# Four blocks of 256 channels for the modulation's shift and scale, with the first two products run beside them

## The chip, the cores and the metric

The kernel runs on one core of a Trainium2 chip. The metric is the device time of one launch in microseconds (us). The kernel before took 747.63 us in the median of 3 runs (746.4 to 748.59). The profile shown here is one further execution, of 750.78 us.

## The reference

One layer of a hybrid transformer over 256 latent tokens and 256 context tokens of 1024 channels. What matters here is its beginning; all else (two attentions, a Fourier mix, a convolution, a merge, a mixture of 16 experts) stays as it is.

```
m  = silu(c) @ w_mod + b_mod              # 6 x 1024 columns: sh1, sc1, g1, sh2, sc2, g2
mc = silu(c_ctx) @ w_mod + b_mod          # the same for the context tokens
h  = rms_norm(x,   norm1_g) * (1 + sc1)  + sh1
hc = rms_norm(ctx, norm1_g) * (1 + csc1) + csh1
gq, gk, gv, nq, nk, nv, fu, cu, gl = split(h @ w_in)      # w_in: 1024 x 7936, products of 256 columns each
```

So the shift `sh1` and the scale `sc1` need the first 2048 columns of `w_mod`, over all 1024 rows (8 MB in 32 bits). The two products `gq` (512 columns of `w_in`, two pieces of 256) are the first that read `h`.

## The kernel before

All of `h` lies transposed: 8 channel tiles k of 128 channels, each with 256 tokens. Every product of the first part runs in three passes with high and low parts: `h` is split by ScalarE (cast, `hhi`) and VectorE (difference, `hlo`), and a weight tile of 1 MB (8 channel tiles by 256 columns) likewise, in two halves of four channel tiles (`stream`, lines 266 to 278; lines 275 and 276 are the cast and the difference). A product of 256 columns is 48 matmuls of 256 columns: 2 halves of the tokens, 8 channel tiles, 3 passes.

The weights come on SyncE's DMA queue (SP), one issue of 1 MB at a time, into a pool `wp` of 4 buffers. An issue waits until its buffer is free, and whatever stands behind it on SP waits too. The constants (`pk`) and `x` (`xs`) come on ScalarE's DMA queue at the same time. A scheduler puts each engine's instructions into a fixed order before the run; an engine waits at the head of its order.

The beginning: `mod_set(0)` (lines 157 to 176) loads the 2048 columns in 8 tiles of 128 rows with 2048 columns (line 162), and adds for each tile 4 matmuls of 512 columns that sit side by side in the four column groups of TensorE (line 164). Only after the eighth tile is the sum complete. Then it is copied out (line 169), turned by 4 transposes (line 172), the bias is added (line 174), and `sh1` and `a1` (which is norm1_g times one plus the scale) come out for all 8 channel tiles at once (lines 248 and 249). `turned_norm` has by then normalized `x` (line 216) and transposed it (line 221). `modulated` (lines 228 to 241) makes `h` channel tile by channel tile: VectorE for the even tiles (line 235), ScalarE for the odd ones (line 237), the cast (line 238), the difference (line 239). The weights of the first `gq` product are loaded behind the 8 tiles; GpSimd makes their low parts. The two `gq` products (line 388) follow, then the context tokens are loaded, normalized, turned and modulated (line 391), then the product `gkv` of both kinds of tokens, and `cb`, `ca`, `nk` and so on.

`side_work` runs one step of `rest_of_mod` after each product from the second on: each step loads another 1 MB of `w_mod` (`wv`, line 184), and VectorE adds it up (lines 190 and 192).

Of the kernel before, what the change touches and what calls it, by code (L numbers as in the profile page):

```python
# [9 lines left out]
F32 = mybir.dt.float32  # L10
F32R = mybir.dt.float32r
# [3 lines left out]
ALU = mybir.AluOpType  # L15
# [37 lines left out]
def mixer_moe(ctx: ExitStack, tc: tile.TileContext, A, out, dbg=None):  # L53
    nc = tc.nc
    V, SC, G, PE = nc.vector, nc.scalar, nc.gpsimd, nc.tensor

    def dump(name, ap):
        if dbg is not None and name in dbg:
            nc.gpsimd.dma_start(dbg[name], ap)
# [12 lines left out]
    def pt(tag, name):  # L72
        return banks["pool"].tile([P, 512], F32, tag=tag, bufs=banks["n"][tag], name=name)
# [7 lines left out]
    def tr_t(name):  # L81
        return pt("tr", name)
# [46 lines left out]
    def big(name, dt=F32):  # L129
        return hp.tile([P, 2048], dt, tag="h", name=name)  # L130
# [21 lines left out]
    V.scalar_tensor_tensor(cth, cth, 1.0, cc, op0=ALU.add, op1=ALU.mult)  # L152
    V.tensor_scalar_mul(csil[:, :, 0:2], cth, 0.5)

    bm = pks("bm").rearrange("p (s j b) -> p s j b", s=3, j=4)

    def mod_set(s, out):

        acc = pt("md", f"mod{s}")
        for k in range(NK):  # L160
            wm = wp.tile([P, 2048], F32, tag="w", name=f"wm{s}_{k}")
            nc.sync.dma_start(wm, A["w_mod"][k * P : (k + 1) * P, 2048 * s : 2048 * (s + 1)])
            for j in range(4):
                PE.matmul(acc[32 * j : 32 * j + 32, :], csil[:, k, :], wm[:, 512 * j : 512 * (j + 1)],
                          start=(k == 0), stop=(k == NK - 1))
            yield
        m = t2(f"m{s}")
        for h in range(2):
            (V.tensor_copy if h else SC.copy)(m[:, 256 * h : 256 * h + 256], acc[:, 256 * h : 256 * h + 256])
        t = tr_t(f"mt_{s}")  # L170
        for b in range(4):
            PE.transpose(t[:, 128 * b : 128 * (b + 1)], m[:, 128 * b : 128 * (b + 1)], ident)
        mt = small.tile([P, 4, 4, 2], F32, name=f"mc_{s}", tag="mc", bufs=2)
        V.tensor_tensor(mt.rearrange("p j b r -> p b j r"), t.rearrange("p (b j r) -> p b j r", b=4, j=4)[:, :, :, 0:2],
                        bm[:, s].rearrange("p j b -> p b j").unsqueeze(3).to_broadcast([P, 4, 4, 2]), op=ALU.add)
        out.append(mt)

    def mod_sums(i, res):

# [48 lines left out]
    def modulated(xT, r, name):

        hi = big(f"hhi{name}", F32R).rearrange("p (k t) -> p k t", k=NK)  # L230
        lo = big(f"hlo{name}", F32R).rearrange("p (k t) -> p k t", k=NK)
        for k in range(NK):
            f = xT[:, k, :]
            if k % 2 == 0:
                V.tensor_scalar(f, f, a1[:, k, r : r + 1], sh1[:, k, r : r + 1], op0=ALU.mult, op1=ALU.add)
            else:
                SC.activation(f, f, AF.Identity, scale=a1[:, k, r : r + 1], bias=sh1[:, k, r : r + 1])
            SC.copy(hi[:, k, :], f)
            V.tensor_sub(lo[:, k, :], f, hi[:, k, :].bitcast(F32))
        dump(f"h{name}", hi.bitcast(F32))  # L240
        H.append((hi, lo))

    xlT = turned_norm(xs, big("xn").rearrange("p (t d) -> p t d", t=NT), big("xTl"), "l")
    mc = []
    for _ in mod_set(0, mc):
        pass
    mc0 = mc.pop()
    V.tensor_copy(sh1, mc0[:, 0:2].rearrange("p j b r -> p (j b) r"))
    V.scalar_tensor_tensor(a1, mc0[:, 2:4].rearrange("p j b r -> p (j b) r"), 1.0,
                           pks("n1g").unsqueeze(2).to_broadcast([P, NK, 2]), op0=ALU.add, op1=ALU.mult)  # L250


    aside = []
# [40 lines left out]
    def tok_major(X, t):  # L294
        return lambda k, w, xi: (X[xi][:, k, 128 * t : 128 * (t + 1)], w)
# [1004 lines left out]
```

## Time and profile before

| what | before |
|---|---|
| median of 3 runs | 747.63 us (746.4 to 748.59) |
| profiled execution, its span | 750.78 us, 749.0 us |
| TensorE matmul busy | 643.1 us (86%) |
| VectorE busy | 414.1 us (55%) |
| ScalarE busy | 265.8 us (35%) |
| GpSimd busy | 71.0 us (9%) |
| moved by DMA | 180.06 MB, mean 240 GB/s |
| granted TensorE clock, mean | 0.942 |

How to read it: a row of a timeline has the start in us from the span's start, the duration in us, the engine, the line of the kernel, the operation, what it writes and reads, the count, and in brackets the engine's idle time before it with what ended it. Neighbouring instructions of one kind are merged into a row. PE is TensorE, PEld its weight loads, DVE VectorE, ACT ScalarE, POOL GpSimd, SP SyncE; a q behind a name is its queue. A granted clock of 1.00 is 2.4 GHz, 0.50 is 1.2 GHz. Buffer numbers are left out of names, so `gq` stands for both products and `wm` for all tiles of `w_mod`.

### The profile page before, as it was taken

Reading aid. Unit: us, or ns where it says so; the run is one execution under the profiler, and the core shown is the slowest. Engines: PE = TensorE matmul, PEld = TensorE weight load, DVE = VectorE, ACT = ScalarE, POOL = GpSimd, SP = SyncE. Lnnn points to the kernel's source line nnn. Section 1 sums busy time; section 2 is a strip of 40 time slices with the busy share of each in tenths; the row PEclk is TensorE's granted clock in tenths of the full one; section 3 lists DMA queues with packets and bytes.
Section 4 is the critical chain, followed back from the end, with each engine's and each line's share of the span. In section 5 each row is a group of like instructions: output and inputs, shape, how many; then the busy total and the mean of one; then the engine's idle time right before and its main releaser. Section 6 shows DMA issues by size and latency. Waiting matters only on the chain. (4 is left out here: it accounts for less than half of the span.)

```text
span 749.0 us, 12068 instructions
## 1 busy us (share of the span) xinstructions
PE 643.1 (86%) x4725; PEld 444.3 (59%) x4725; DVE 414.1 (55%) x806; ACT 265.8 (35%) x486; POOL 71.0 (9%) x112
## 2 busy tenths in 40 slices
PE   3689899999999999999999686879789778797882
PEld 0278899978887999898999522423224224232221
DVE  0279799988988766775666523431324324304233
ACT  1157845367556343434545311220102112201011
POOL 1134200022111002112120100000000000000000
PEclk9979999999999999999999878989899999999995
DMA  9895653542624878577984608999658999966002
GB/s 365 295 330 158 194 171 113 180 158 71 205 85 163 295 254 265 198 249 258 320 296 171 225 1 322 408 407 408 257 226 359 406 408 408 381 246 267 1 2 87
DMA packets 75119, 180.06 MB, mean 240 GB/s; under 512 B 3104, under 2 KB 39072, under 8 KB 74016
## 3 DMA queue, kind: packets, MB, share of 16 engines
q1 hardware_dynamic: 73088, 172.90, 63.3%
q0 software_dynamic: 1104, 3.15, 1.3%
q10 hardware_dynamic: 848, 2.94, 1.0%
q8 instruction: 52, 0.85, 0.5%
q14 instruction: 27, 0.22, 0.1%
HBM read 177.92 MB, written 1.05 MB: 239 GB/s over the span
## 5 line engine op out<-in xcount | busy, mean ns | idle before, releaser
L810 PE MATMUL gu<-we,hg 128*32 128x512 f32 x832 | 111.0, 655 | 3.2 <-PEq L1125 3.2
L288 PE MATMUL gl<-hhil,wl_gl 128*128 128x256 f32 x256 | 72.8, 286 | 1.5 <-DVE wl_gl L276 1.4
L810 PEld LDWEIGHTS gu<-we,hg 128*32 128x32 f32 x832 | 29.6, 117 | 74.2 <-issue 71.4
L288 PE MATMUL gl<-hhil,wh_gl 128*128 128x256 f32 x256 | 73.4, 287 | 0.0
L288 PE MATMUL gl<-hlol,wh_gl 128*128 128x256 f32 x256 | 72.4, 283 | 0.0
L456 DVE SCALAR_TENSOR_TENSOR cv<-zp,pk,cv 128x256 f32<-128x256 f32 x120 | 51.2, 477 | 0.2
L275 ACT CAST wh_gl<-w_gl 128x1024 fp32r<-128x1024 f32 x32 | 33.1, 1048 | 50.0 <-PE gl L288 25.2
L810 PE MATMUL y<-we,hT 128*32 128x512 f32 x416 | 49.6, 607 | 0.9 <-PEq L1176 0.8
L288 PEld LDWEIGHTS gl<-hhil,wl_gl 128*128 128x128 f32 x256 | 48.1, 189 | 3.7 <-DVE wl_gl L276 3.1
L288 PEld LDWEIGHTS gl<-hhil,wh_gl 128*128 128x128 f32 x256 | 48.1, 188 | 1.6 <-issue 1.6
L288 PEld LDWEIGHTS gl<-hlol,wh_gl 128*128 128x128 f32 x256 | 48.2, 188 | 0.5 <-issue 0.5
L288 PE MATMUL z<-y,wh_br 128*128 128x256 f32 x256 | 47.6, 283 | 0.0
L276 DVE TENSOR_TENSOR wl_gl<-w_gl,wh_gl 128x1024 fp32r<-128x1024 f32 x32 | 41.0, 1294 | 9.8 <-ACT wh_gl L275 9.6
L192 DVE SCALAR_TENSOR_TENSOR acc<-wv,csil,acc 128x512 f32<-128x512 f32 x56 | 41.1, 762 | 6.5 <-DMA wv<-in_w_mod_dram 6.4
L288 PEld LDWEIGHTS z<-y,wh_br 128*128 128x128 f32 x256 | 39.6, 188 | 0.9 <-issue 0.7
L874 DVE TENSOR_TENSOR si<-si,gu 128x256 f32<-128x256 f32 x16 | 6.6, 418 | 59.4 <-ACT si L873 59.3
L288 PE MATMUL z<-y,wl_br 128*128 128x256 f32 x128 | 36.8, 289 | 1.8 <-DVE wl_br L276 1.7
L372 ACT CAST yh<-ys 64x512 fp32r<-64x512 f32 x32 | 19.7, 616 | 46.3 <-DVE ys L892 45.7
L873 ACT ACTIVATE si<-gu 128x256 f32<-128x256 f32 x16 | 6.0, 383 | 84.1 <-PE gu L810 65.7
L810 PEld LDWEIGHTS y<-we,hT 128*32 128x32 f32 x416 | 14.2, 111 | 31.3 <-issue 29.5
L892 DVE SCALAR_TENSOR_TENSOR ys<-y,gsl,G 128x512 f32<-128x512 f32 x16 | 12.0, 751 | 34.6 <-PE y L810 31.2
L672 POOL TENSOR_TENSOR merged<-merged,gt 128x512 f32<-128x512 f32 x12 | 19.3, 1610 | 117.6 <-DVE gt L671 117.6
(411 smaller groups left out, 1525.5 us busy)
## 6 DMA issues: line engine op xcount, KB each, us to landing
we<-in_w_gu_dram SPq DMA_DIRECT2D x64, 1024.0 KB, 9.7
we<-in_w_down_dram SPq DMA_DIRECT2D x32, 1024.0 KB, 15.8
wv<-in_w_mod_dram SPq DMA_DIRECT2D x16, 1024.0 KB, 5.5
w_gl<-in_w_in_dram SPq DMA_DIRECT2D x16, 1024.0 KB, 5.6
wm<-in_w_mod_dram SPq DMA_DIRECT2D x8, 1024.0 KB, 9.4
w_br<-in_w_branch_dram SPq DMA_DIRECT2D x8, 1024.0 KB, 5.2
w_out<-in_w_out_dram SPq DMA_DIRECT2D x4, 1024.0 KB, 5.4
w_gq<-in_w_in_dram SPq DMA_DIRECT2D x2, 1024.0 KB, 8.3
```

What stands on the lines that cost most here:

```text
L192: V.scalar_tensor_tensor(acc[:, s], wm[:, k % 2, s], csil[:, k, 0:1], acc[:, s], op0=ALU.mult, op1=ALU.add)
L275: SC.copy(w[0], raw[:, s])
L276: sub(w[1], raw[:, s], w[0].bitcast(F32), op=ALU.subtract)
L288: PE.matmul(dst, a, b, start=(k == 0 and wi + xi == 0), stop=(k == kt - 1 and wi == 1))
L372: SC.copy(hi, src)
L456: V.scalar_tensor_tensor(cv[:, ct, :], zp[:, ct, j : j + S], convw[:, ct, j : j + 1], cv[:, ct, :], op0=ALU.mult, op1=ALU.add)
L672: G.tensor_tensor(mt, mt, gts[c], op=ALU.add)
L810: tc.keep_in_program_order(PE.matmul(*a, **k))
L873: SC.activation(si, acc[:, :n], AF.Silu)
L874: V.tensor_tensor(si, si, acc[:, n:], op=ALU.mult)
L892: V.scalar_tensor_tensor(ys, y, gsl, G2[flip], op0=ALU.mult, op1=ALU.mult)
```

## The change

The shift and the scale are made in four blocks of 256 channels (two channel tiles). A block b loads two tiles: the 256 shift columns and the 256 scale columns, over all 1024 rows (`mod_load`, the same 1 MB each, now in pieces of 1 KB per row instead of 8 KB). `mod_product` runs 32 matmuls of 128 columns into the four column groups where 4 per tile of 512 columns ran before (128 matmuls in all where there were 32, for the same columns), and VectorE copies 128 columns out. `mod_turn` transposes once and writes two channel tiles of `sh1` and `a1` with three small VectorE operations. `modulated` is called for these two channel tiles. The two `gq` products are cut up by channel tiles: `first_products(c, ks)` adds the channel tiles ks of product c, for tiles of `h` that were made one block earlier, and the last two channel tiles come at the end. Each of the four accumulators (2 pieces of columns, 2 halves of tokens) now has a bank of its own, three of the pool `mm`, one of `sc`. The second product's weights lie in two buffers of the pool `h` (`wide`). The loads of the two `gq` weight tiles stand behind block 0 and block 1. The counter that starts `side_work` is set to 2 by hand, so that the first step of `rest_of_mod` comes after `gkv`.

```diff
+    def mod_load(b):
+        ws = []
+        for i in range(2):
+            wm = wp.tile([P, 2048], F32, tag="w", name=f"wm{b}_{i}").rearrange("p (k n) -> p k n", k=NK)
+            c = D * i + 2 * P * b
+            nc.sync.dma_start(wm, A["w_mod"][:, c : c + 2 * P].rearrange("(k p) n -> p k n", p=P))
+            ws.append(wm)
+        return ws
+
+    def mod_product(b, ws):
+        acc = pt("md", f"mod{b}")
         for k in range(NK):
-            wm = wp.tile([P, 2048], F32, tag="w", name=f"wm{s}_{k}")
-            nc.sync.dma_start(wm, A["w_mod"][k * P : (k + 1) * P, 2048 * s : 2048 * (s + 1)])
-            for j in range(4):
-                PE.matmul(acc[32 * j : 32 * j + 32, :], csil[:, k, :], wm[:, 512 * j : 512 * (j + 1)],
+            for g in range(4):
+                PE.matmul(acc[32 * g : 32 * g + 32, :P], csil[:, k, :], ws[g // 2][:, k, P * (g % 2) : P * (g % 2) + P],
                           start=(k == 0), stop=(k == NK - 1))
+        m = t2(f"m{b}")
+        V.tensor_copy(m[:, :P], acc[:, :P])
+        return m
+
+    def mod_turn(b, m):
+        t = tr_t(f"mt_{b}")
+        PE.transpose(t[:, :P], m[:, :P], ident)
...
+        V.tensor_tensor(sh1[:, k, :], t[:, 0], bias[:, 0, k].unsqueeze(2).to_broadcast([P, 2, 2]), op=ALU.add)
+        V.tensor_tensor(mt, t[:, 1], bias[:, 1, k].unsqueeze(2).to_broadcast([P, 2, 2]), op=ALU.add)
+        V.scalar_tensor_tensor(a1[:, k, :], mt, 1.0, pks("n1g")[:, k].unsqueeze(2).to_broadcast([P, 2, 2]),
+                               op0=ALU.add, op1=ALU.mult)
...
-    ws0 = stream(A["w_in"][:, :256], NK, "gq0", G.tensor_tensor)
-    modulated(xlT, 0, "l")
+    new_h("l")
+    gq = [[(sc_t if 2 * c + t == 3 else mm_t)(f"gq{c}{t}")[:, :256] for t in range(NT)] for c in range(2)]
+    gws = []
+
+    def first_products(c, ks):
+        for t in range(NT):
+            for k in ks:
+                w = gws[c][2 * k // NK]
+                for wi, xi in ((0, 0), (0, 1), (1, 0)):
+                    a, b = tok_major(H[0], t)(k, w[wi][:, k % 4, :], xi)
+                    PE.matmul(gq[c][t], a, b, start=(k == 0 and wi + xi == 0), stop=(k == NK - 1 and wi == 1))
+
+    for b in range(4):
+        m = mod_product(b, mod_load(b))
+        if b:
+            first_products(0, range(2 * b - 2, 2 * b))
+        mod_turn(b, m)
+        if b < 2:
+            gws.append(stream(A["w_in"][:, 256 * b : 256 * b + 256], NK, f"gq{b}", V.tensor_tensor if b else G.tensor_tensor, b == 1))
+        modulated(xlT, 0, range(2 * b, 2 * b + 2))
+        if b:
+            first_products(1, range(2 * b - 2, 2 * b))
+    for c in range(2):
+        first_products(c, range(6, NK))
+    n_prod[0] = 2
...
-    gq = [in_cols(256 * c, f"gq{c}", tok_major, ws=None if c else ws0)[0] for c in range(2)]
...
-    modulated(turned_norm(ctxs, ctxs, big("xTc"), "c"), 1, "c")
+    new_h("c")
+    modulated(turned_norm(ctxs, ctxs, big("xTc"), "c"), 1, range(NK))
```

What the change moves on the engines is shown at three places. First SyncE's queue from its start. Before, the eight tiles of `w_mod` go ahead of both `gq` weight tiles, one tile of `wv` and the context tokens (`wm0_3` is the fourth tile):

```order
L162 DMA wm0_0_141<-in_w_mod_dram 128x2048
L162 DMA wm0_1_147<-in_w_mod_dram 128x2048
...
L162 DMA wm0_7_183<-in_w_mod_dram 128x2048
L270 DMA w_gq0_201<-in_w_in_dram 128x8x256
L270 DMA w_gq1_297<-in_w_in_dram 128x8x256
L184 DMA wv4_0_356<-in_w_mod_dram 128x2x1024
L390 DMA ctxs_360<-in_ctx_dram 128x2x1024
L270 DMA w_gkv_491<-in_w_in_dram 128x8x256
```

Now (`wm3_1` is the scale tile of block 3):

```order
L161 DMA wm0_0_146<-in_w_mod_dram 128x8x256
L161 DMA wm0_1_148<-in_w_mod_dram 128x8x256
L273 DMA w_gq0_191<-in_w_in_dram 128x8x256
L161 DMA wm1_0_207<-in_w_mod_dram 128x8x256
L161 DMA wm1_1_209<-in_w_mod_dram 128x8x256
L273 DMA w_gq1_264<-in_w_in_dram 128x8x256
L161 DMA wm2_0_290<-in_w_mod_dram 128x8x256
L161 DMA wm2_1_292<-in_w_mod_dram 128x8x256
L161 DMA wm3_0_365<-in_w_mod_dram 128x8x256
L161 DMA wm3_1_367<-in_w_mod_dram 128x8x256
L420 DMA ctxs_474<-in_ctx_dram 128x2x1024
L273 DMA w_gkv_605<-in_w_in_dram 128x8x256
```

The last tile that the modulation needs is now the tenth transfer and not the eighth; both `gq` weight tiles are ahead of it, and one tile of `wv` has gone behind `gkv`.

Second TensorE, from the end of the modulation's sum. Before, the whole of the first product stands behind the turn `mt_0`:

```order
L164 MATMUL mod0_140<-wm0_6_177,csil_102 32x512 x4
L164 MATMUL mod0_140<-wm0_7_183,csil_102 32x512 x4
L172 MATMUL mt_0_192<-pk_67,m0_189 128x128 x4
L288 MATMUL gq0_0_247<-wh_gq00_203,hhil_211 128x256
L288 MATMUL gq0_0_247<-wh_gq00_203,hlol_212 128x256
```

Now, around the turn of the last block (`gq11` is the second piece of columns for the second half of the tokens; the rows in between go on in the same way), up to `gkv`:

```order
L170 MATMUL mod3_369<-wm3_1_367,csil_102 32x128 x2
L327 MATMUL gq10_144<-wl_gq1_267,hhil_140 128x256
...
L327 MATMUL gq11_145<-wh_gq1_266,hhil_140 128x256
L178 MATMUL mt_3_416<-pk_67,m3_402 128x128
...
L231 MATMUL xtrc0_487<-pk_67,ctxs_474 128x128
L231 MATMUL xtrc1_493<-pk_67,ctxs_474 128x128
L327 MATMUL gq00_142<-wh_gq01_197,hlol_141 128x256
...
L231 MATMUL xtrc0_487<-pk_67,ctxs_474 128x128 x3
L231 MATMUL xtrc1_493<-pk_67,ctxs_474 128x128 x3
L293 MATMUL gkv_0_603<-wh_gkv0_607,hhil_140 128x256
```

Behind the last matmul of block 3 stand 30 matmuls of the `gq` products, and the first two transposes of the context tokens are among them, ahead of the last 8.

Third VectorE. Before, all of `h`'s low parts come in one row, with `wv` behind:

```order
L249 SCALAR_TENSOR_TENSOR a1_71<-mc_0_197,pk_67 128x16
L235 TENSOR_SCALAR xTl_107<-xTl_107,a1_71,sh1_72 128x256 x4
L239 TENSOR_TENSOR hlol_212<-xTl_107,hhil_211 128x256 x7
L190 TENSOR_SCALAR acc4_355<-wv4_0_356,csil_102 128x512
```

Now, for the last block (`ctxs` are the context tokens):

```order
L173 COPY m3_402<-mod3_369 128x128
L182 TENSOR_TENSOR sh1_72<-mt_3_416,pk_67 128x4
L184 TENSOR_TENSOR mc_3_419<-mt_3_416,pk_67 128x4
L185 SCALAR_TENSOR_TENSOR a1_71<-mc_3_419,pk_67 128x4
L247 TENSOR_SCALAR xTl_107<-xTl_107,a1_71,sh1_72 128x256
L251 TENSOR_TENSOR hlol_141<-xTl_107,hhil_140 128x256
L226 TENSOR_SCALAR ctxs_474<-ctxs_474,rsc_482 128x1024
L251 TENSOR_TENSOR hlol_141<-xTl_107,hhil_140 128x256
L226 TENSOR_SCALAR ctxs_474<-ctxs_474,rsc_482 128x1024
L281 TENSOR_TENSOR wl_gkv0_608<-w_gkv_605,wh_gkv0_607 128x1024
```

The scaling of the context tokens stands between the low parts of the last two channel tiles, and the four additions of the first `wv` tile are no longer in this stretch.

## Rows read from the trace of the kernel before

**Rows 1.** Windows: stretch, its length, busy us of each engine, clock, DMA share, GB/s.

```profile
0.00:5.00 5.00, 0.00 (x0) 0.00 (x0) 0.27 (x1) 1.28 (x1) 0.45 (x7) 1.00 0.64 202
15.00:20.00 5.00, 1.92 (x2) 0.18 (x2) 0.62 (x1) 2.19 (x4) 1.96 (x5) 1.00 1.02 424
22.00:24.00 2.00, 2.00 (x12) 1.14 (x6) 0.14 (x1) 0.00 (x0) 0.00 (x0) 1.00 0.23 53
44.00:47.50 3.50, 3.50 (x18) 3.50 (x18) 3.50 (x7) 0.72 (x2) 0.00 (x0) 0.50 1.09 347
100.00:150.00 50.00, 50.00 (x412) 49.00 (x410) 48.65 (x103) 23.47 (x34) 1.40 (x2) 1.00 0.47 153
```

**Rows 2.** Waits of TensorE from 56 to 430 us, the longest: total us, times, longest.

```profile
PE cum L775 <- DVE mask L768: 4.3, 1, 4.3
```

**Rows 3.** TensorE's timeline, from the modulation's end to `cb`.

```profile
25.20 1.09 PE L221 MATMUL xtrl<-pk,xn 128*128 128x128 f32 x8
...
32.44 1.06 PE L164 MATMUL mod<-wm,csil 128*32 128x512 f32 x8 [2.58 <-DMA wm<-in_w_mod_dram]
...
37.59 0.58 PE L288 MATMUL gq<-wh_gq,hhil 128*128 128x256 f32 x1 [2.45 <-ACT hhil L238]
...
44.39 0.41 PE L288 MATMUL gq<-wh_gq,hhil 128*128 128x256 f32 x1
...
45.03 0.41 PE L288 MATMUL gq<-wh_gq,hhil 128*128 128x256 f32 x1
...
55.31 0.28 PE L288 MATMUL gq<-wh_gq,hhil 128*128 128x256 f32 x1
...
55.66 0.28 PE L288 MATMUL gq<-wh_gq,hhil 128*128 128x256 f32 x1
...
56.80 0.36 PE L288 MATMUL gkv<-wh_gkv,hhil 128*128 128x256 f32 x1
...
70.97 0.28 PE L288 MATMUL cb<-hhil,wh_cb 128*128 128x256 f32 x1
```

**Rows 4.** DMA issues of the first 60 us: KB, us from issue to landing.

```profile
xs<-in_x_dram ACTq DMA_DIRECT2D x1, 1024.0 KB, 14.5
...
w_gkv<-in_w_in_dram SPq DMA_DIRECT2D x1, 1024.0 KB, 14.2
pk<-in_pk_dram ACTq DMA_DIRECT2D x1, 823.0 KB, 7.6
```

**Rows 5.** DMA queues from 3 to 8 us (q1 SP's, q10 ScalarE's): packets, MB, share.

```profile
q1 hardware_dynamic: 164, 1.21, 58.2%
q10 hardware_dynamic: 158, 0.88, 42.4%
```

**Rows 6.** SyncE's queue in the timeline.

```profile
33.57 0.48 SPq L270 DMA_DIRECT2D w_gkv<-in_w_in_dram  x1
```

**Rows 7.** ScalarE's timeline.

```profile
43.57 1.06 ACT L212 ACTIVATE xTc<-ctxs 128x1024 f32<-128x1024 f32 x1 [0.52 <-DMA ctxs<-in_ctx_dram]
...
57.78 1.10 ACT L237 ACTIVATE xTc<-xTc,sh,a 128x256 f32<-128x256 f32 x2
...
59.27 1.33 ACT L238 CAST hhic<-xTc 128x256 fp32r<-128x256 f32 x4
```

**Rows 8.** VectorE's timeline.

```profile
35.18 0.19 DVE L174 TENSOR_TENSOR mc<-mt,pk 128x32 f32<-128x32 f32 x1 [0.78 <-PE mt L172]
...
52.79 1.42 DVE L216 TENSOR_SCALAR ctxs<-ctxs,rsc 128x1024 f32<-128x1024 f32 x2 [0.93 <-POOL rsc L111]
...
54.52 2.47 DVE L276 TENSOR_TENSOR wl_gkv<-w_gkv,wh_gkv 128x1024 fp32r<-128x1024 f32 x2
...
62.55 1.42 DVE L239 TENSOR_TENSOR hloc<-xTc,hhic 128x256 fp32r<-128x256 f32 x4
```

**Rows 9.** GpSimd's timeline.

```profile
37.31 4.86 POOL L276 TENSOR_TENSOR wl_gq<-w_gq,wh_gq 128x1024 fp32r<-128x1024 f32 x2 [15.80 <-ACT wh_gq L275]
...
52.01 0.74 POOL L111 TENSOR_TENSOR rsc<-rsc,pk 128x2 f32<-128x2 f32 x1
```

More of the change, by code (lines that the diff above doesn't have):

```diff
@@ L153, in mixer_moe @@
     V.tensor_scalar_mul(csil[:, :, 0:2], cth, 0.5)
-    bm = pks("bm").rearrange("p (s j b) -> p s j b", s=3, j=4)
-    def mod_set(s, out):
-        acc = pt("md", f"mod{s}")
+    def mod_load(b):
[6 more added lines that the diff above has]
+        return ws
@@ L165, in mod_set @@
                           start=(k == 0), stop=(k == NK - 1))
[L166 to L175, printed above, removed]
@@ L176, in mod_set @@
-        out.append(mt)
+        m = t2(f"m{b}")
[4 more added lines that the diff above has]
+        PE.transpose(t[:, :P], m[:, :P], ident)
+        t = t[:, :P].rearrange("p (i c r) -> p i c r", i=2, c=2)[:, :, :, 0:2]
+        k = slice(2 * b, 2 * b + 2)
+        bias = pks("bm").rearrange("p (s k) -> p s k", s=6)
+        V.tensor_tensor(sh1[:, k, :], t[:, 0], bias[:, 0, k].unsqueeze(2).to_broadcast([P, 2, 2]), op=ALU.add)
+        mt = small.tile([P, 2, 2], F32, name=f"mc_{b}", tag="mc", bufs=2)
+        V.tensor_tensor(mt, t[:, 1], bias[:, 1, k].unsqueeze(2).to_broadcast([P, 2, 2]), op=ALU.add)
+        V.scalar_tensor_tensor(a1[:, k, :], mt, 1.0, pks("n1g")[:, k].unsqueeze(2).to_broadcast([P, 2, 2]),
+                               op0=ALU.add, op1=ALU.mult)
@@ L226, in mixer_moe, with new_h, modulated @@
     H = []
[L228 to L232, printed above, removed]
+    def new_h(name):
+        H.append([big(f"h{v}{name}", F32R).rearrange("p (k t) -> p k t", k=NK) for v in ("hi", "lo")])
+    def modulated(xT, r, ks):
+        hi, lo = H[r]
+        for k in ks:
             f = xT[:, k, :]
@@ L239, in modulated @@
             V.tensor_sub(lo[:, k, :], f, hi[:, k, :].bitcast(F32))
-        dump(f"h{name}", hi.bitcast(F32))
-        H.append((hi, lo))
     xlT = turned_norm(xs, big("xn").rearrange("p (t d) -> p t d", t=NT), big("xTl"), "l")
[L244 to L250, printed above, removed]
     aside = []
@@ L264, in side_work, with stream @@
                         break
-    def stream(src, kt, name, sub=V.tensor_tensor):
+    def stream(src, kt, name, sub=V.tensor_tensor, wide=False):
         raw = wp.tile([P, 2048], F32, tag="w", name=f"w_{name}")
@@ L271, in stream @@
         ws = []
+        if wide:
+            wide = [big(f"w{c}_{name}", F32R) for c in "hl"]
         for q in range(2):
             s = slice(1024 * q, 1024 * (q + 1))
-            w = [hl.tile([P, 1024], F32R, tag="hl", name=f"w{c}_{name}{q}") for c in "hl"]
+            w = [v[:, s] for v in wide] if wide else [hl.tile([P, 1024], F32R, tag="hl", name=f"w{c}_{name}{q}") for c in "hl"]
             SC.copy(w[0], raw[:, s])
@@ L308, in halves @@
         return acc.rearrange("p (c q) -> p c q", c=2)
-    ws0 = stream(A["w_in"][:, :256], NK, "gq0", G.tensor_tensor)
-    modulated(xlT, 0, "l")
+    new_h("l")
[3 more added lines that the diff above has]
+        for t in range(NT):
+            for k in ks:
+                w = gws[c][2 * k // NK]
+                for wi, xi in ((0, 0), (0, 1), (1, 0)):
+                    a, b = tok_major(H[0], t)(k, w[wi][:, k % 4, :], xi)
+                    PE.matmul(gq[c][t], a, b, start=(k == 0 and wi + xi == 0),
+                              stop=(k == NK - 1 and wi == 1))
+    for b in range(4):
[11 more added lines that the diff above has]
+    n_prod[0] = 2
     ropec = pks("ropec").rearrange("p (t d) -> p t d", t=NT)
@@ L394, in mixer_moe @@
         for c in range(2):
-            SC.copy(qq[:, 4 * c : 4 * c + 4, :], gq[c][:, 256 * t : 256 * t + 256].rearrange("p (h d) -> p h d", h=4))
+            SC.copy(qq[:, 4 * c : 4 * c + 4, :], gq[c][t].rearrange("p (h d) -> p h d", h=4))
         head_rstd(qs[:, t, :], qq, NH, f"q{t}")
```

## Prediction

> **What bounds the kernel now.** I read the windows first, since one share of busy time over the whole span mixes stages. From 100 to 150 us TensorE is busy in all 50 us and VectorE in 48.65, while DMA is at 0.47 [rows 1]; the waits of TensorE say that from 56 to 430 us it stood still in one place for 4.3 us and nowhere else for more than 1.7 in sum [rows 2]. So from the first products on, whatever lets TensorE start earlier lets it end earlier, as long as VectorE keeps up. The beginning is another regime. The matmul timeline shows the modulation's last tile landing at 32.44, the first `gq` matmul at 37.59, `gkv` at 56.80 and `cb` at 70.97 [rows 3]. From 37.59 to 56.80 lie 96 matmuls that take 0.213 us each at the half clock (three in 0.64, from 44.39 to 45.03) and 0.117 at the full one (three in 0.35, from 55.31) [rows 3]; at the full clock the 96 would take 11.2 us, so about 8 us of this stretch are waits and clock, and before it TensorE waited for 8 MB. DMA was no constant stream there: from 22 to 24 us it moved 53 GB/s [rows 1], because the next tile's buffer was still being read by matmuls queued behind the transposes of `x`.
>
> **The change, part by part.** I follow the one chain that decides: the last modulation tile, W.
>
> *When W lands.* The first 5 us moved 202 GB/s, about 1.0 MB, against 424 at full flow [rows 1], so flow starts at 5.0 - 1.0/0.424 = 2.6 us. Ahead of W lie `pk` and `xs`, 0.84 + 1.05 MB [rows 4], 4.5 us at 424 GB/s, and ten tiles of 1.05 MB on SP, now all in pieces of 1 KB. For 8 KB pieces the rows show 424 GB/s, for the 1 KB pieces of `w_in` 347 [rows 1]. `w_mod` in 1 KB pieces is not in this trace; I take 347, so 3.02 us a tile and 30.2 in all: W = 37.3 us, against 32.4 for the last tile before. From one side 424 for the eight tiles (W = 32.9); from the other, the same loss once more, 283 GB/s (W = 42.7).
>
> This needs an unbroken stream. The tile `wm2_0` waits for the buffer of `w_gq0`, so for GpSimd's 4.86 us of low parts [rows 9]: `w_gq0` lands near 16, two casts go ahead, and the buffer is free near 22, while transfers already issued last to 25. `wm3_1` waits for VectorE's two low parts of `w_gq1` (2.47 us [rows 8]), which stand behind the turn of block 1 and that behind 12 `gq` matmuls: near 30.6, while the transfers issued last to 34.2. Behind each of the two on SP stand all later loads, so these margins of 3 us are what covers the new waits; were one gone, W would move by the excess.
>
> *The x chain.* From 3 to 8 us the two queues moved 164 and 158 packets, 1.21 and 0.88 MB [rows 5]: they alternate packet by packet, and SP's were 8 KB. With 1 KB on SP, `pk` and `xs` get most of the flow, and `xs`, which landed at 1.2 + 14.5 = 15.7 [rows 4], should land near 8.5. The norm then waits for nothing but the copy of block 0, and the first block of `h` is ready near 24. If `xs` still came at 15.7, block 0 would be ready near 29 and W would slip by about 1.2, no more.
>
> The Trainium skill, page "DMA: Bandwidth & Descriptors", section "Queues, rings and completion order", says that an engine drains a whole packet of typically 9 to 17 descriptors before it turns to another queue. The counts above show alternation, and do not show how many pieces went into a turn; by the rule with turns of equal bytes, `xs` would land near 12, which changes W by nothing.
>
> *From W to `gkv`.* Block 3's matmuls: the same columns as 8 matmuls of 512, which took 1.06 us at 32.44; 32 one after the other like the transposes (8 in 1.09) would be 4.4 [rows 3]. I take 2.0, nearer to the four column groups side by side. Copy 0.3, turn and the four matmuls ahead of it 0.5, three small VectorE operations 0.5 (each at most 0.19 [rows 8]): `a1` at W + 3.3. The even channel tile on VectorE 0.4, its cast 0.33, the odd one on ScalarE 0.55, then ScalarE's second square of the context tokens (1.06 and a read-out), then the cast: W + 6.1 [rows 7]. GpSimd's root near 1.0 with its 0.74 power [rows 9], VectorE's half of the scaling 0.71, low part 0.4 [rows 8]: W + 8.0. The last 8 `gq` matmuls 0.9, second half of the scaling and 6 transposes of 0.136: `gkv` starts at W + 9.9 = 47.2 us. Before it was 56.80: 9.6 us earlier. The weights are there: two tiles after W (context 2.6, `gkv` 3.0) is 42.9, where `gkv` landed at 33.57 + 14.2 = 47.8 [rows 4, 6]. The 96 `gq` matmuls lie mostly under the stream; only the 30 behind block 3 are on this chain, and most of those under ScalarE's and VectorE's work.
>
> *From `gkv` to `cb`.* Here something is given back. Before, VectorE took from 52.79 to 63.97 for scaling, weights' low parts and all of `hc`, 11.2 us [rows 8], and TensorE had 48 `gkv` matmuls of the latent tokens to do meanwhile. Now the scaling starts at W + 6.9 = 44.2, that work lasts to 55.4, and the low part of `gkv`'s second half stands at its end (the order has it behind most of `hc`). TensorE has only 28 of the 96 matmuls to do until then. The other 68 at 0.117, with four turns of `q`, take 8.4: `cb` at 63.9, against 70.97, so 7.1 us earlier. VectorE's four moved `wv` additions (about 2.4 us, before in idle time) come into its crowded stretch, but `rest_of_mod` now runs one product later throughout and ends where VectorE waits anyway; I charge 0.1 for it.
>
> *Small parts.* 96 more matmuls and weight loads, and 12 more small VectorE operations, lie under the stream except for block 3's, counted above. The two extra `h` buffers and the fourth bank: no load or matmul in the order waits for them before `cb`. I set them at nothing; if the bank held up `gkv`, it would be by one copy, 0.4.
>
> Sum: 7.1 - 0.1 = 7.0 us. The profiled execution goes from 750.78 to 743.8 (span 749.0 to 742.0). It lies 3.15 above the median of the runs shown, so the median goes from 747.63 to 740.6.
>
> **The rivals.**
>
> *The clock stays low.* From 44 to 47.5 us TensorE was wholly busy and had 0.50 [rows 1]. In the new beginning its work comes in pieces between waits, so it may stay at 1.2 GHz until `gkv`. The 30 matmuls behind block 3 then cost 30 x 0.096 = 2.9 more and block 3 itself 2.0 more; not all of it is under ScalarE's work: 2.5 to 4.9 less gain, a median of 743.1 to 745.5. For it: before, ten microseconds after the first product it still had not risen [rows 1, 3]. Against it: between 24 and 40 TensorE has 72 `gq` matmuls and three blocks, 8.4 + 6.0 us of work in 16.
>
> The Trainium skill, page "TensorE: Matmul & The Clock Gate", section "Part 1: The HAM clock gate", calls the low level the default that activity releases. The row above agrees that 1.2 GHz was held at the start of steady work; what it would be worth here is this rival's price.
>
> *More comes through.* The gap of TensorE in front of the second half of `gkv` is filled, because VectorE is earlier than I have it, and the 9.6 us come through whole, perhaps with W some microseconds earlier: a gain of 9.5 to 12, 735.6 to 738.1. For it: `w_mod` at 424. Against it: VectorE's 11.2 us are a row.
>
> *It does not come through.* VectorE, busy in 48.65 of 50 us [rows 1], is the true bound between 60 and 150, and the earlier start only makes TensorE wait there: a gain under 2.2. Against it: TensorE's waits after 56 us are so few [rows 2], and VectorE starts earlier too.
>
> *Slower.* The eight `w_mod` tiles in 1 KB pieces run much below `w_in`'s, since every piece jumps to another row of a 24 KB pitch. At 250 GB/s they take 33.6 us, with the two `gq` tiles and the start W = 46.7, and the time is 9.4 worse than forecast: 750.0. It decides from 270 GB/s, where W = 44.3 and nothing is gained. For it: eight times as many pieces. Against it: `w_in` with a pitch of 31 KB has 347.
>
> **How the numbers follow.** Forecast (a gain of 4.9 to 9.5, 738.1 to 742.7): 0.60. More: 0.13. Low clock: 0.13. Not through: 0.07. Slower: 0.07. A difference under 0.3%, 2.2 us, could not be told from none here. Faster by more: 0.60 + 0.13 + 0.12 = 0.85; same 0.08; slower 0.07. The range leaves out the slower case and most of the one that does not come through: 735.8 to 745.6.
>
> **What would show it.** In the changed kernel's trace: the scale tile of block 3 lands at 37 (33 to 43) and DMA has no gap before it; `xs` is squared near 9; the first `gq` matmul is near 24; `gkv` starts near 47 and `cb` near 64, with a wait of TensorE for `wl_gkv` in between; from there on every stage is 6 to 8 us earlier, up to the end. I am wrong if DMA idles between 20 and 37, if tiles of `w_mod` take over 3.8 us each, if the clock is 0.50 up to 50 us, or if the lead at `cb` shrinks before 430 us.

## The result, and the profile after

The changed kernel is slower. Beside the shown runs of the kernel before it took 755.56 us against 747.76 (medians of 4 runs each; ratio 1.0099, interval 1.0072 to 1.0127). In later runs it took 752.17 (12 runs) against 747.19 (35 runs): ratio 1.0070, interval 1.0046 to 1.0095. So it loses 5 to 8 us where a gain of 7.0 was forecast. The profiled execution below took 753.02 us (span 751.2), the lowest of its four; the one of before took 750.78, some 3 us above its medians. So stage times say more here than the two spans.

The windows of the changed kernel, in the columns of [rows 1]; the next to last line is the stretch from the first `gkv` matmul to the first `ca` matmul:

```profile
10.00:25.00 15.00, 8.12 (x82) 6.01 (x82) 5.02 (x5) 4.50 (x7) 7.70 (x9) 0.84 1.10 348
28.00:30.00 2.00, 2.00 (x30) 1.80 (x18) 0.63 (x3) 1.76 (x2) 0.00 (x0) 1.00 0.33 85
53.71:90.30 36.59, 30.39 (x215) 28.27 (x214) 30.39 (x78) 27.88 (x69) 15.78 (x14) 0.91 0.46 148
85.00:89.00 4.00, 3.94 (x21) 3.65 (x20) 3.35 (x8) 2.48 (x10) 0.00 (x0) 0.57 1.00 338
```

And the stretch from `gkv` to `ca` in the kernel before:

```profile
56.80:85.90 29.10, 26.20 (x215) 25.19 (x214) 26.78 (x68) 24.28 (x61) 11.11 (x13) 1.00 0.49 151
```

TensorE's timeline after, the places of [rows 3]. L170 is the modulation, L327 the first products, L293 all later ones. `wh_` and `wl_` are the high and low parts of a product's weights, `hhil` and `hlol` those of `h`, `hhic` and `hloc` those of `hc`:

```profile
26.08 2.36 PE L170 MATMUL mod<-wm,csil 128*32 128x128 f32 x60
28.37 0.39 PE L327 MATMUL gq<-wh_gq,hhil 128*128 128x256 f32 x1
...
37.48 0.28 PE L327 MATMUL gq<-wl_gq,hhil 128*128 128x256 f32 x1
37.68 1.94 PE L170 MATMUL mod<-wm,csil 128*32 128x128 f32 x60
...
41.85 0.74 PE L327 MATMUL gq<-wh_gq,hhil 128*128 128x256 f32 x4 [0.99 <-ACT hhil L250]
...
44.18 1.94 PE L170 MATMUL mod<-wm,csil 128*32 128x128 f32 x60
...
53.71 0.37 PE L293 MATMUL gkv<-wh_gkv,hhil 128*128 128x256 f32 x1
...
61.45 0.58 PE L293 MATMUL gkv<-wl_gkv,hhil 128*128 128x256 f32 x1 [1.93 <-DVE wl_gkv L281]
61.83 0.41 PE L293 MATMUL gkv<-wh_gkv,hhil 128*128 128x256 f32 x1
62.05 0.41 PE L293 MATMUL gkv<-wh_gkv,hlol 128*128 128x256 f32 x1
...
71.37 0.28 PE L293 MATMUL cb<-hhil,wh_cb 128*128 128x256 f32 x1
...
90.32 0.28 PE L293 MATMUL ca<-hhil,wh_ca 128*128 128x256 f32 x1
```

VectorE, GpSimd and SyncE's queue after (`xn` is the normalized `x`, `ctxs` the context tokens):

```profile
17.56 3.55 DVE L226 TENSOR_SCALAR xn<-xs,rsl 128x1024 f32<-128x1024 f32 x2
...
52.60 1.22 DVE L281 TENSOR_TENSOR wl_gkv<-w_gkv,wh_gkv 128x1024 fp32r<-128x1024 f32 x1
...
60.18 1.22 DVE L281 TENSOR_TENSOR wl_gkv<-w_gkv,wh_gkv 128x1024 fp32r<-128x1024 f32 x1
```

```profile
18.22 5.11 POOL L281 TENSOR_TENSOR wl_gq<-w_gq,wh_gq 128x1024 fp32r<-128x1024 f32 x2 [3.55 <-ACT wh_gq L280]
```

```profile
61.46 0.37 SPq L194 DMA_DIRECT2D wv<-in_w_mod_dram  x1
69.84 0.37 SPq L273 DMA_DIRECT2D w_ca<-in_w_in_dram  x1
```

How to read them. The first product starts 9.2 us earlier (28.37 for 37.59) and `gkv` 3.1 earlier (53.71 for 56.80), but `cb` is 0.4 later (71.37 for 70.97) and `ca` 4.4 later (90.3 for 85.9). So the start is faster and the stretch from `gkv` to `ca` takes 36.6 us instead of 29.1. With 215 matmuls recorded in both, it has 6.2 us of TensorE idle instead of 2.9, and part of it runs at 1.2 GHz (0.91 on average for 1.00). In the order [rows 8] both halves of the low part of `gkv`'s weights were one row, 54.52, ahead of all of `hc`. Now they are two, 7.6 us apart, with most of `hc` between them; TensorE stands 1.93 us for the second, and the matmuls behind it are 0.22 apart, the half clock. The next `wv` tile on SyncE's queue waited for the same split (11.7 us), and `w_ca` behind it for another 8.3 us until VectorE had written `qr`: issued at 57.0 before, it came at 69.84.

Theories: **A**, the blocks form a serial loop on TensorE, since each block's modulation matmuls stand behind `gq` matmuls of the block before, which wait for its `h`; **B**, the late second split of `gkv`'s weights; **C**, the `wv0` additions that moved behind `gkv`; **D**, GpSimd's split of `gq0`'s weights, now beside `xn`, slows VectorE (3.55 us for 1.80).

### The profile page after: what moved, and what is told of

Same layout as the page of the kernel before. It is cut to its first block, busy times and chain, and to the rows that moved or that the text cites. A ratio compares the mean times of both kernels' runs of the same rounds, so it can differ in the third digit from the quotient of the medians.

```text
span 751.2 us, 12461 instructions
## 1 busy us (share of the span) xinstructions
PE 646.5 (86%) x4917; PEld 454.3 (60%) x4917; DVE 414.9 (55%) x818; ACT 265.7 (35%) x485; POOL 76.8 (10%) x112
## 3 DMA queue, kind: packets, MB, share of 16 engines
q1 hardware_dynamic: 80256, 172.90, 63.7%
## 5 line engine op out<-in xcount | busy, mean ns | idle before, releaser
L293 PE MATMUL gl<-hhil,wl_gl 128*128 128x256 f32 x256 | 73.8, 291 | 1.6 <-DVE wl_gl L281 1.5
L293 PE MATMUL gl<-hhil,wh_gl 128*128 128x256 f32 x256 | 74.4, 291 | 0.0
L293 PE MATMUL gl<-hlol,wh_gl 128*128 128x256 f32 x256 | 73.4, 287 | 0.0
L293 PEld LDWEIGHTS gl<-hhil,wl_gl 128*128 128x128 f32 x256 | 49.2, 193 | 3.7 <-DVE wl_gl L281 3.2
L293 PEld LDWEIGHTS gl<-hhil,wh_gl 128*128 128x128 f32 x256 | 49.3, 193 | 2.0 <-issue 2.0
L293 PEld LDWEIGHTS gl<-hlol,wh_gl 128*128 128x128 f32 x256 | 49.4, 193 | 0.9 <-issue 0.9
L281 DVE TENSOR_TENSOR wl_gl<-w_gl,wh_gl 128x1024 fp32r<-128x1024 f32 x32 | 43.0, 1360 | 8.0 <-ACT wh_gl L280 7.9
L293 PE MATMUL z<-y,wh_br 128*128 128x256 f32 x256 | 47.4, 283 | 0.0
L293 PEld LDWEIGHTS z<-y,wh_br 128*128 128x128 f32 x256 | 39.5, 188 | 0.5 <-issue 0.5
L293 PE MATMUL z<-y,wl_br 128*128 128x256 f32 x128 | 36.7, 288 | 0.1
L841 PEld LDWEIGHTS y<-we,hT 128*32 128x32 f32 x416 | 14.2, 111 | 30.9 <-issue 29.3
L703 POOL TENSOR_TENSOR merged<-merged,gt 128x512 f32<-128x512 f32 x12 | 19.1, 1591 | 118.8 <-DVE gt L702 118.8
```

The lines of the kernel that those rows point to most:

```text
L293: PE.matmul(dst, a, b, start=(k == 0 and wi + xi == 0), stop=(k == kt - 1 and wi == 1))
L703: G.tensor_tensor(mt, mt, gts[c], op=ALU.add)
L841: tc.keep_in_program_order(PE.matmul(*a, **k))
```

## The experiments

All ratios are to runs of the kernel before on the same chip. e1 to e4 ran on one chip, where the kernel before had a median of 747.37, e5 to e12 on another, where it had 747.19 (e5 to e8) and 748.11 (e9 to e12). So a difference in us between two of these groups carries up to 0.9 us that is not the kernel's. The expectations of e1 to e4 count from the first 755.56 of the changed kernel, and later runs of it took 752.17. The columns behind the ratio are from one trace each (us); those of the changed kernel are from e5's.

| kernel | median | ratio (95%) | `gkv` starts | `gkv` to `cb` | `gkv` to `ca` |
|---|---|---|---|---|---|
| before | 747.2 to 748.1 | | 56.8 | 14.2 | 29.1 |
| changed | 752.17 | 1.0070 (1.0046 to 1.0095) | 52.2 | 17.9 | 37.0 |
| e1 products alone | 758.77 | 1.0155 (1.0132 to 1.0177) | 57.6 | 13.4 | 30.6 |
| e2 modulation first | 744.68 | 0.9954 (0.9931 to 0.9977) | 50.5 | 13.2 | 27.9 |
| e3 `gkv` split early | 745.77 | 0.9975 (0.9949 to 1.0002) | 51.5 | 13.1 | 27.4 |
| e4 side work early | 749.90 | 1.0047 (1.0023 to 1.0072) | 56.8 | 22.2 | 36.9 |
| e6 e2, split late | 749.08 | 1.0025 (0.9996 to 1.0054) | 51.9 | 20.1 | 33.9 |
| e7 `gq0` on VectorE | 749.05 | 1.0032 (1.0011 to 1.0054) | 49.1 | 18.8 | 36.5 |
| e8 e2 and e7 | 745.61 | 0.9981 (0.9959 to 1.0003) | 50.3 | 13.3 | 28.0 |
| e9 blocks alone | 746.92 | 0.9967 (0.9944 to 0.9990) | 55.5 | 13.4 | 28.6 |
| e10 before, split late | 752.12 | 1.0057 (1.0033 to 1.0081) | 57.4 | 22.5 | 37.1 |
| e11 e3 and e7 | 742.97 | 0.9918 (0.9886 to 0.9951) | 50.0 | 13.2 | 27.4 |
| e12 e11, turns first | 742.39 | 0.9911 (0.9880 to 0.9943) | 49.4 | 13.1 | 27.2 |

In the changed kernel, e4, e6, e7 and e10 the second split of `gkv`'s weights is late, in the others early. Up to `cb` the two groups are apart: 17.7 (the first trace of the changed kernel) to 22.5 us against 13.1 to 14.2. Each late one has a stretch at 1.2 GHz inside `gkv`, of some 3 to 13 us, and no early one has.

**e1, the second half of the change alone.** The modulation as before; both weight tiles streamed early, products by pairs:

```
+gws = [stream(.., "gq0", G.tensor_tensor), stream(.., "gq1", wide=True)]
+for b in range(4):
+    modulated(xlT, 0, range(2 * b, 2 * b + 2))
+    for c in range(2): first_products(c, range(2 * b, 2 * b + 2))
```

> The modulation is computed as in the kernel before (eight tiles of 2048 columns, one turn), and only the second half of the change stands: both weight tiles of the first two products are split early and their matmuls run by pairs of channel tiles behind h, the weights of gq1 in wide tiles. Theory A (the block by block modulation is what costs, because each block's matmuls on TensorE wait behind the products of the block before): h is complete at 46 as in the kernel before, the last gq matmul falls near 49 to 51 (before 56.0, after 53.2), gkv starts near 51 to 54, ca near 84 to 87, and the time is 745 to 748. Theory B (the instruction order behind the first two products, with the second half of gkv's weights behind the context tokens' h and q's chain behind it, is what costs): gkv is early too, but gkv to ca takes 35 to 37 us as in the changed kernel (before 29.1), ca near 89, time 750 to 755.

Neither: 758.77, worse than both theories had it. `gkv` came no earlier (57.6). `gkv` to `ca` is only 30.6, but there `ca` begins while `cb` still runs (till 94.3), and up to the next product at 105.7 the stretch takes 48.1 us, as long as in the changed kernel (48.1) and longer than before (42.0). TensorE's waits of 50 to 110 us in e1:

```profile
PE cb L283 <- ACT wh_cb L270: 2.3, 3, 0.9
PE cb L283 <- DVE wl_cb L271: 1.1, 1, 1.1
```

It looks like the same illness in another place: `cb`'s second weight half is cast only at 72.51 and subtracted at 75.61, after `cb` began at 71.0, and a stretch at half clock follows. No run mended that, so e1's cause is argued and not shown. A's forecast for it (745 to 748) failed, and it decides nothing between A and B.

**e2, modulation first.** Only TensorE's order is asked for, but the order of the other engines followed: in it, both halves of `wl_gkv` stand together again.

```
+with tc.issue_after(last_mod[b]):
     first_products(..)
```

> The changed kernel with the first products of block b-1 made to stand behind the modulation matmuls of block b on TensorE; nothing else is changed. Theory A (those matmuls wait behind gq, and h with them): modulation of block 2 near 34 to 35 (37.7 in the changed kernel), of block 3 near 40 to 41 (44.2), last hlo near 48 (52.0), gkv near 50.5 (53.7), and at least half of the 3 us reaches ca: time 752 to 753.5. Theory B (the order behind the products costs, and the start of gkv doesn't set ca): h and gkv come 3 us earlier all the same, ca stays within 1 us of 90.3, time 754.5 to 756.5.

744.68: 7.5 us better than the changed kernel, far more than A expected. The last low part of `h` starts at 47.9 (51.6 in the changed kernel), `gkv` starts at 50.5, `cb` at 63.7. The block's matmuls now wait for data alone:

```profile
34.17 1.94 PE L172 MATMUL mod<-wm,csil 128*32 128x128 f32 x60 [1.13 <-DMA wm<-in_w_mod_dram]
...
40.09 1.94 PE L172 MATMUL mod<-wm,csil 128*32 128x128 f32 x60 [0.49 <-DMA wm<-in_w_mod_dram]
```

With two things changed at once, it doesn't tell A from B; e3 and e6 do.

**e3, `gkv`'s split early**, TensorE's blocks as in the changed kernel.

```
+ws_kv = stream(A["w_in"][:, 512:768], NK, "gkv")
 modulated(turned_norm(ctxs, ..), 1, range(NK))
...
-gkv = in_cols(512, "gkv", tok_major, (0, 1))
+gkv = in_cols(512, "gkv", tok_major, (0, 1), ws=ws_kv)
```

> The changed kernel with the load and the splits of gkv's weights placed in the code ahead of the context tokens' h, as far as the order is concerned; nothing else is changed. Theory B (the second half of wl_gkv behind hc on VectorE makes TensorE idle 1.93 us at 59.5, and the 14 matmuls behind it run at half clock, 1.4 us): both go, cb near 68.5 to 69.5 (71.4), and if nothing else holds it ca near 87.5, time 752 to 753.5. Theory A (only the late h matters): gkv still starts at 53.7, the wait moves to hloc instead and the time stays 754.5 to 756.5.

745.77, 6.4 us better than the changed kernel: B, and more than B's own figure, since `gkv` to `cb` (13.1 for 17.7) and `cb` to `ca` (14.3 for 18.9) both shrink. Its window from `gkv` to `ca`, and one behind it:

```profile
51.50:78.90 27.40, 25.71 (x212) 24.88 (x211) 25.44 (x64) 22.63 (x54) 14.54 (x12) 1.00 0.54 174
84.00:90.00 6.00, 5.88 (x28) 5.88 (x28) 4.54 (x9) 2.44 (x7) 0.00 (x0) 0.51 1.04 335
```

e3 too has a stretch at half clock near 85 us, behind the start of its `ca`. So `ca` flatters it: `ca` starts 11.4 us earlier than in the first trace of the changed kernel, `gl`, the last product on `h`, 6.0 (198.2 for 204.2), which is near the 6.4 of the medians.

**e4, side work early.**

```
+side_work()
 ctxs = big("ctxs")...
```

> The changed kernel with the first step of the side work (load of wv0 and its four additions on VectorE) back ahead of the load of the context tokens, where it stood before the change. Theory C (these four additions, moved behind gkv, lag VectorE by 3 to 4 us between 60 and 85 and with it q's chain and ca): cb to ca goes from 18.9 back to 15 to 16, ca 86.5 to 87.5, time 751.5 to 753. Theories A and B: the additions only trade places with splits that TensorE waits for, ca within 1 us of 90.3, time 754 to 757; later context tokens on the queue may even add 1 to 2 us.

Unclear on C: 749.90, 2.3 us better than the changed kernel and below both forecasts. The twelve runs spread from 746.2 to 757.1, and the traced one was the slowest: the context tokens, now behind `wv0` on the queue, came late, TensorE stood at half clock from 55 to 68 us and waited 4.2 us for `wl_gkv`. `cb` to `ca` is 14.7 as C had it, but `gkv` to `ca` is 36.9, so C is neither shown nor ruled out.

**e5, the changed kernel again**, for a second trace.

> The changed kernel, unaltered, for a second trace and more times beside the variants: 753 to 757. In its first trace TensorE stood at half clock from 20.9 to 27, from 33.7 to 37.2, from 61 to 65 and from 85 to 90 us, while the variant with gkv's weights placed earlier, whose instructions are the same in the first 33 us, stood at half clock only from 22 to 25 there. If the idle times alone set these stretches, the second trace shows the same four; if the moments at which the clock falls differ from execution to execution, the first two move or vanish and h comes up to 2 us earlier in this trace, without the run being more than 2 us faster.

752.17, a little less than expected, traced at 749.32. Two of the four half-clock stretches are gone (20 to 28 and 33 to 37.5 us), two stand where they stood. The first trace:

```profile
20.00:28.00 8.00, 6.83 (x75) 5.11 (x77) 3.73 (x9) 2.52 (x6) 3.33 (x2) 0.57 1.09 346
33.00:37.50 4.50, 4.17 (x24) 3.90 (x23) 0.99 (x3) 0.41 (x1) 0.00 (x0) 0.62 1.09 347
61.00:65.00 4.00, 3.55 (x18) 3.55 (x19) 4.00 (x11) 1.37 (x4) 3.83 (x3) 0.57 0.61 181
84.00:90.00 6.00, 5.59 (x33) 5.30 (x34) 3.76 (x9) 4.45 (x12) 0.85 (x1) 0.72 0.86 298
```

The second:

```profile
20.00:28.00 8.00, 6.50 (x75) 4.85 (x77) 3.72 (x8) 2.19 (x5) 3.66 (x2) 1.00 1.08 348
33.00:37.50 4.50, 4.16 (x74) 3.76 (x77) 0.97 (x3) 0.41 (x1) 0.00 (x0) 1.00 1.10 347
61.00:65.00 4.00, 4.00 (x25) 4.00 (x24) 3.32 (x8) 0.00 (x0) 3.75 (x4) 0.61 0.76 255
84.00:90.00 6.00, 5.69 (x36) 5.66 (x36) 4.17 (x7) 3.78 (x10) 0.00 (x0) 0.72 0.60 207
```

So the first two are chance of the execution, worth 1.5 us of `gkv` (52.2 for 53.7). One like the third, inside `gkv`, is in every trace with the split late. The fourth doesn't follow the split: e2, e3 and e8, with the split early, have it between 82 and 90 us too, and e7, with the split late, has not. `gkv` to `ca` is 37.0 in this trace too.

**e6, e2 with the split put back late.**

```
+with tc.issue_after(last_lo[-2]):   # gkv, second half: behind 7 of 8 hloc
     sub(w[1], raw[:, s], ..)
```

> The variant in which the modulation matmuls of a block stand ahead of the products of the block before (744.7), with one thing put back as it was in the changed kernel: the second half of gkv's weight split on VectorE stands behind seven of the eight hloc subtractions. Theory A (late h by the order on TensorE is the cause): gkv still near 50.5, cb at most 1.5 us later than 63.7, time 745 to 747. Theory B (the place of that split on VectorE is the larger cause: TensorE waits for it, then runs at half clock, and the load of wv1 and the weights behind it wait too): gkv near 50.5 but gkv to cb 16 to 18 us as in the changed kernel (13.2 in the variant), cb near 67 to 68, ca near 84 to 86, time 749 to 753.

749.08: B. With A's cure kept, the late split alone costs 4.4 us. Beside the changed kernel, where the split is late as well, A's cure is worth 3.1. `gkv` to `cb` is 20.1, more than B had; TensorE's longest wait:

```profile
PE gkv L302 <- DVE wl_gkv L288: 3.1, 1, 3.1
```

**e7, `gq0`'s split on VectorE** in the changed kernel, and **e8** the same in e2.

```
-V.tensor_tensor if b else G.tensor_tensor, b == 1
+V.tensor_tensor, b == 1
```

> The changed kernel with the split of gq0's weights on VectorE instead of GpSimd; it comes behind the scaling xn there. Theory D (GpSimd's split beside it slows VectorE, xn x2 3.55 us instead of 1.80, and that delays the first turn): xn takes 1.8 to 1.9 us, the transposes xtrl start at 19.5 instead of 21.2 and the first a1 is there by 25 to 25.5 (26.45) even with 2.4 us of splits on VectorE; h 1 us earlier, time 753 to 755. If GpSimd has nothing to do with it, xn stays at 3.5 us and the 2.4 us of splits come on top: time 756 to 759. Theory B: wl_gkv's second half is as late as before in this order, so most of the 8 us of loss remain in either case.

> Modulation matmuls ahead of the products of the block before (744.7), and gq0's weights split on VectorE instead of GpSimd. Theory D: xn 1.8 instead of 3.5 us, first a1 1 us earlier; but blocks 2 and 3 stood behind their data there (TensorE waited 1.1 and 0.5 us for wm2 and wm3), so only what the earlier release of those tiles gives comes through: 743 to 745. If VectorE's splits delay the copies of xTl instead: 745 to 747.

D holds. In e7 `xn` takes 1.41 us, with 2.4 us of splits behind it, and the first `a1` is there at 23.53 instead of 26.45:

```profile
18.00 1.41 DVE L226 TENSOR_SCALAR xn<-xs,rsl 128x1024 f32<-128x1024 f32 x2
19.32 1.22 DVE L281 TENSOR_TENSOR wl_gq<-w_gq,wh_gq 128x1024 fp32r<-128x1024 f32 x1
...
23.53 0.16 DVE L185 SCALAR_TENSOR_TENSOR a<-mc,pk 128x4 f32<-128x4 f32 x1
```

e7 is 3.1 us better than the changed kernel and still slower than before: `gkv` starts at 49.1, the earliest of all, and 36.5 us up to `ca` follow. In e8, where blocks wait for data, nothing comes of it: 745.61 beside 744.68, in the range of the other forecast; but its trace stood at half clock from 21 to 28 us, so which of the two holds is open. The Trainium skill, page "Perfetto Trace Analysis", section "Optimizing Scalar/DVE Operations", says that GpSimd and VectorE share an SBUF read port, so that moving work between them might not help. The trace agrees that the two hold each other up, 3.55 and 3.49 us for `xn` beside the split and 1.41 without; the port itself no run here shows, and moving the split to VectorE did help, by the 3.1 us of e7.

**e9, blocks alone**, whole products behind them. **e10, the kernel before with the late split** (the edit of e6).

> The first half of the change alone: the modulation by blocks of 256 channels and h block by block, but the two products whole behind the last block, as in the kernel before. In its order both halves of wl_gkv stand ahead of hc on VectorE. Theory A (what costs is the serial loop of block and products): without products between the blocks, h is complete near 47 to 48 as in the variant with the modulation first, but the 96 matmuls of gq then stand behind it and take 11.3 us at full clock, gkv near 60, ca near 88 to 90, time 750 to 753. Theory B (the late split of gkv's weights costs): gkv to cb 13 to 14.5, gkv to ca 27.5 to 29, so ca near 87 to 89 and 749 to 751. The two differ in gkv to ca: 35 or more by the first, below 30 by the second.

> The kernel before the change with one thing altered: the second half of gkv's weight split on VectorE is put behind seven of the eight hloc subtractions, as it stands in the changed kernel. Theory B: gkv to cb grows from 14.2 to 17 to 20 us, gkv to ca from 29.1 to 33 to 37, the time from 747.2 to 751 to 754. Theory A: there is slack for it in this kernel, gkv to cb at most 15.5, the time 746.5 to 748.5.

Both speak for B. e9, whose order has the split early, gains 1.2 us (ratio below 1) with `gkv` to `ca` at 28.6, where A had 35 or more; its time is better than either theory had it. e10 turns the kernel before into one as slow as the changed one, 4.0 us worse, by this one edit. Its window from `gkv` to `ca`, and TensorE's longest wait in it:

```profile
57.40:94.50 37.10, 29.24 (x216) 27.55 (x215) 29.42 (x72) 27.09 (x67) 9.78 (x14) 0.91 0.45 144
```

```profile
63.54 0.58 PE L294 MATMUL gkv<-wh_gkv,hhic 128*128 128x256 f32 x1 [3.27 <-ACT qq L401]
```

The scheduler rebuilt the other engines' order around it. TensorE waits only 0.8 us for `wl_gkv` there, and 3.3 for ScalarE's copies of the `gq` results (`qq`). So it is shown that the late split costs; by which wait it does so depends on the order.

**e11, e3 and e7 together; e12, with modulation matmuls and turns ahead of the products as well.**

> The changed kernel with gkv's weights loaded and split ahead of the context tokens' h, and gq0's weights split on VectorE; TensorE's order of blocks and products is the changed kernel's. Theories B and D add: 3 us of the earlier start seen with VectorE alone (752.2 to 749.1) and 6 to 8 us of the earlier split (745.8): gkv near 48, gkv to ca near 27.5, time 741.5 to 744. If VectorE, with less slack, gives the 3 us back between gkv and ca: 744.5 to 746.5.

> As the one before, and with both the modulation matmuls and the turn of a block ahead of the products of the block before on TensorE. Theory A: h isn't behind the products at all then; the blocks are held by the data alone (wm3 landed near 40 in these kernels), a turn comes 1.4 us after its block instead of 1.5 to 2, gkv near 47 to 49 and time 740 to 743. If the order on TensorE no longer matters once the split is early, the same as the one before within 1.5 us.

742.97 and 742.39: both beat the kernel before, e12 by 0.9%, and by the two ratios the changed one by 1.6% (0.9911/1.0070). B and D add: 6.4 and 3.1 us alone, 9.2 together. With both mended the change lies inside the range that was forecast, 2 us above the forecast itself. A adds 0.6 us once they are cured, which is no difference here. e12's DMA has no gap any more (28 to 30 us), and its stretch from `gkv` to `ca` is the shortest:

```profile
28.00:30.00 2.00, 1.80 (x15) 1.60 (x14) 2.00 (x2) 1.35 (x4) 0.00 (x0) 1.00 1.07 347
49.40:76.60 27.20, 25.36 (x212) 24.78 (x211) 25.43 (x63) 22.38 (x52) 10.93 (x10) 1.00 0.58 186
```

## Why the prediction was wrong

By its own terms: `gkv` was to start at 47.2 and started at 53.7 (6.5 late), `gkv` to `cb` was to take 16.7 and took 17.7 (1.0), and `cb` to `ca` was to take 14.9 as before and took 18.9 (4.0). These 11.5 us turn the 7.1 of gain into the 4.4 of loss at `ca`. So two steps failed: the one that makes a loss of the change, and, larger in us, the start of block 3.

*The step that makes the loss: "Here something is given back", from `gkv` to `cb`.* The place was seen (the second low part behind most of `hc`, TensorE waiting for it), and up to `cb` the size was nearly right: the wait was to end 8.2 us behind the start of `gkv` and ended after 7.7, and the matmuls from there to `cb` were to take 8.4 us and took 9.9, the first of them at half clock. Wrong was to charge 2.5 us and let it end at `cb`. Measured up to `ca`, the stretch is 36.6 and 37.0 us in the two traces against 29.1, so 7.5 to 7.9. In every kernel with that split late the stretch is 33.9 to 37.1, in every one with it early, e1 left out, 27.2 to 29.1. In time the split is worth 6.4 us in the changed kernel (e3; 7.1 by the ratios), 4.4 in e2's order (e6; 5.3), 4.0 in the kernel before (e10; 4.3). Without it the change is no loss: 745.77.

Where the price falls differs. From `cb` to `ca` only the changed kernel and e7, which has its order, are long (18.9, 19.1 and 17.6 us); e4, e6 and e10 have 13.7 to 14.7 there and pay more before `cb`. In the changed kernel's trace the rest, beyond the 1.93 us of waiting, shows as matmuls at half clock behind the gap, later waits for `qr`, `kn` and `wl_cb` (1.1, 1.9 and 0.8 us for 0.8, 1.1 and none before), and a second stretch at half clock before `ca`, which other orders have without the late split. Which of these follows from which wasn't separated.

*The start: "W = 37.3".* `xs` came near the forecast (landing at 9.7 for 8.5), the 1 KB pieces of `w_mod` ran at 348 GB/s as assumed, and from block 3's matmuls to `gkv` it took 9.5 us (forecast 9.9, counted from the landing). Block 3's matmuls took 1.94 (2.0), which is partly luck: the row of 1.06 us that was read as 8 matmuls of 512 is one tile, 4 matmuls that stand in the trace twice each, and a block has two. Wrong was when block 3 ran: 44.2 instead of 37.3. In e2 its data was there at 40.1, since the margins "near 22" and "near 30.6" left out the tiles that wait for block 1's own matmuls. These ended at 28.4 behind the transposes of `x`, which waited for `xn`, slowed by GpSimd; hence the gap of 85 GB/s, which e7, e11 and e12, without that split on GpSimd, don't have (344 to 348). The kernel before had shown the price. Beside the same split, 37.31 in [rows 9], seven low parts of `h` took 6.57 us, where four of `hc` took 1.42 [rows 8]:

```profile
37.57 6.57 DVE L239 TENSOR_TENSOR hlol<-xTl,hhil 128x256 fp32r<-128x256 f32 x7 [0.49 <-ACT hhil L238]
```

The remaining 4.1 us are the order on TensorE. The prediction put the `gq` matmuls "mostly under the stream", and did not ask what stands behind them in the same queue.

*From `cb` to the end.* That "whatever lets TensorE start earlier lets it end earlier" held for the loss, the other way round: 4.4 us at `ca` and 4.1 at the start of the MoE's products. For gains it holds in part: in e2 `ca` starts 7.5 us earlier than before, but from there to `nv` it takes 38.8 us instead of 35.9, with 2.1 us of waits for `wl_ca` and a stretch at half clock from 84 us. The rival in which VectorE takes the gain back was the nearest to what happened, but not by its busy share: by what stands in front in its queue. The rival of slow 1 KB pieces did not occur; the one of a low clock did, in one of two traces and for 1.5 us at `gkv`.

## What to carry to other kernels

When an edit moves the moment at which an engine becomes free, the list of every other engine may be rebuilt around it: look up where the preparation of the next product's operands stands, and don't price a late one by its wait alone. Here TensorE stood 1.9 to 4.2 us inside `gkv`, a stretch at half clock went with it each time, and `gkv` to `cb` grew by 3.5 to 8.3. An instruction queued behind others that wait for a later stage inherits their wait, so a loop over blocks on one in-order engine is as long as its longest chain, however early the data lands. Restoring one row of the order, with one split off GpSimd, made of a 0.7% loss a 0.8% gain.

## What the hardware showed

- Two scalings of 128x1024 on VectorE take 1.41 us with GpSimd at rest, 1.80 beside small operations there (the kernel before) and 3.5 beside a subtraction on GpSimd: 0.75 for the one that began ahead of it and 2.89 for the other. The subtraction took 5.1 to 5.5 us; the 4.86 of [rows 9] were beside VectorE's low parts.
- The stretches at 1.2 GHz differ between executions of one program (0.57 and 1.00 from 20 to 28 us in two traces of the changed kernel). Over 89 runs of the kernel before, the time goes with the mean granted clock: at 0.953 and above (19 runs) the median is 744.8 us, at 0.942 and below (13 runs) 749.5. What sets it in a run isn't shown.
